# Cache pages fetched by direct DMAs of SyncE instead of GpSimd's indirect DMAs, and one output tile split into 512 and 64 columns

## The chip, the cores and the metric

One core of a Trainium2 chip runs the whole program. The engines are TensorE (PE; its weight loads are listed apart as PEld), VectorE (DVE), ScalarE (ACT), GpSimd (POOL) and SyncE (SP), which here only issues DMAs. The metric is the device time in microseconds (us); a kernel's time is the median of its runs.

## The reference

Two decoder layers (width 1024) run over 576 tokens: one prompt of 512, and 8 samples of 8 new tokens, each with 1024 past tokens in a paged cache. Cut to what matters here:

```
h = rmsnorm(x, ln_mix)
(hq, hf, hi, hog, dq, dk, dv, gq, gk, gv, gz, gb, ga, gate_a, gate_b, gate_c) = split(h @ w_in)
o_a = gated linear attention of hq, hf, hi          # 4 heads, "hg"
past_k, past_v = cache_k[l, page_table], cache_v[l, page_table]    # samples: 8 pages of 128 rows each
o_b = differential attention of dq, dk, dv over past and new tokens  # 4 heads, "df"; samples "ds"
o_c = gated delta rule of conv(gq, gk, gv)           # 4 heads, "gd"
mix = sigmoid(gate_a) * (o_a @ w_branch_a) + sigmoid(gate_b) * (o_b @ w_branch_b) + sigmoid(gate_c) * (o_c @ w_branch_c)
x = x + mix @ w_out
x = x + (silu(conv(g_ff)) * u_ff) @ w_down           # g_ff, u_ff = split(rmsnorm(x) @ w_up)
```

`page_table` [8, 8] holds numbers of 80 pages. A page of one layer is 128 rows of 512 floats (256 KB), for K (laid out feature by key) and for V. All states, new K and V rows and histories are outputs too.

## The kernel before

Activations lie feature-major: a tile is 128 features by 576 tokens. Every dense product is `dense_steps` (L264): for each of up to 8 tiles of the contraction it issues six matmuls of 288 columns each (weights split into a high and a low part, inputs too; three combinations, two halves of the tokens) into one PSUM accumulator of two banks. Its weights come as `raw` tiles of 128 x 512 floats (256 KB, four contraction tiles), loaded by SP at L274 into four rotating buffers; ACT casts the high part (L261), DVE subtracts for the low part (L194, `wl`). A raw buffer is thus used by 24 matmuls, and its next load waits for DVE's subtraction.

A layer has two parts. In the first, `drive` (L315) interleaves generators on three lanes (left, right and `smp`) with filling products. A generator yields an estimated time (us of planned PE time) after which its next PE step is to be placed, or asks for a dense product. The lanes left and right take the differential heads (df), then the delta-rule (gd) and linear heads (hg). The lane `smp` takes the decays, and after all df heads one `diff_sample` (L1256) per sample, then `diff_finish`. The filling products are eight gates of the heads and 24 branch gates, whose results are stored to DRAM (L716). PE runs in the order that comes of it. Program order and dependencies set the order of the other engines, each of which works strictly in its order; semaphores keep the data safe.

`diff_sample` fetches eight K pages in two tiles `pg` of four pages (two buffers in all, shared with V), multiplies the new keys (`sn`), waits 7.0, multiplies the scores of the first four pages and at once fetches the first four V pages into the buffer that this frees, waits 7.0, does the same for the second four, then the softmax, waits 7.5, transposes (yields 1.0, 1.0, 2.0), multiplies with V (32 matmuls per sample and one more group for the new values), and waits 1.2. Each page is one GpSimd indirect DMA (L1261), whose 128 row numbers stand in `idx` (L619, page number times 128 plus partition). A fetch waits for the matmuls that read the buffer last.

A delta-rule head sends a small tile through DRAM and back (`da`, `dtr`, `dt`, `ctt`, L849 to L864, all on SP). SP also loads states and stores results.

The second part is dense: the merge (L1376), the output projection (`w_out`, L1412), and the feed-forward network, with products of 288 columns throughout.

Of the kernel before, what the change touches and what calls it, by code (L numbers as in the profile page):

```python
# [22 lines left out]
SEQ = 512  # L23
# [122 lines left out]
def kernel(ctx, tc, a, o, depth=DEPTH, dbg=None):  # L146
# [15 lines left out]
    side = ['left']  # L162
    clk = [0.0]
# [32 lines left out]
    def params_load(l):  # L196
        """A layer's small parameters; the second part is loaded by the function that is returned."""
        fm = lay.tile([128, _FMN], F32, tag='fm', bufs=2, name='fm')
        nc.scalar.dma_start(fm, a['p_fm'][l])
        bcp = lay.tile([128, _BCN], F32, tag='bcp', bufs=2, name='bcp')  # L200
        hg = lay.tile([128, 12, 8, 3], F32, tag='hg', bufs=2, name='hg')

        def rest(eng):
            eng.dma_start(bcp, a['p_bc'][l].partition_broadcast(128))
            eng.dma_start(hg, a['hist_g'][l])

        return dict(F={k: fm[:, s:s + n] for k, (s, n) in _FMO.items()},
                    B={k: bcp[:, s:s + n] for k, (s, n) in _BCO.items()}, hg=hg), rest
# [41 lines left out]
    def rsqrt(out, v, n):  # L250
        """out = v ** -0.5 on [128, n] (v is kept)."""
        y, w = out, sm.tile([128, 20], F32, tag='rs_w', name='rs_w')[:, :n]
        V.tensor_scalar(out=y.bitcast(I32), in0=v.bitcast(I32), scalar1=1, scalar2=None, op0=ALU.logical_shift_right)
        V.tensor_scalar(out=y.bitcast(I32), in0=y.bitcast(I32), scalar1=-1, scalar2=0x5F3759DF, op0=ALU.mult, op1=ALU.add)
        for _ in range(3):
            tt(w, y, y, ALU.mult)
            V.scalar_tensor_tensor(out=w, in0=w, scalar=-0.5, in1=v, op0=ALU.mult, op1=ALU.mult)
            V.scalar_tensor_tensor(out=y, in0=w, scalar=1.5, in1=y, op0=ALU.add, op1=ALU.mult)
# [5 lines left out]
    def dense_steps(src, xs, M=128, raws=None, nk=None, prime=False):  # L264
        """src: dram [128, nk * M]; xs: [(xH, xL)] per k tile -> PSUM [M, 2, :288]; yields between k tiles.

        Weights are loaded, and split, ahead of their products; primed, it first yields when those of the first are."""
# [20 lines left out]
        for g, (k0, n) in enumerate(gr):  # L288
            wh, wl = nxt
            for i in range(n):  # L290
                if i == min(1, n - 1) and g + 1 < len(gr):
                    nxt = weights(g + 1)
                xh, xl = xs[k]
                cs = slice(i * M, (i + 1) * M)
                for w, xx in ((wh, (xh, xl)), (wl, (xh,))):
                    for hf in range(2):
                        for x_ in xx:
                            mm(acc[:M, hf, :HALF], w[:, cs], x_[:, hf * HALF:(hf + 1) * HALF],
                               start=(k == 0 and w is wh and x_ is xh), stop=(k == nk - 1 and w is wl))
                k += 1  # L300
                if k < nk:
                    yield
        return acc[:, :, :HALF]

    def dense(src, xs):
        return run(dense_steps(src, xs))
# [8 lines left out]
    def drive(stages, fill, xs, pre, psmp):  # L315
        """Interleaves stages (generators on two lanes) and filling products on the tensor engine.

        A stage yields a time to wait for its operands, ('mm', tile, src) for a product with xs, ('fill', key)
        for a filling product to have been done, or ('done', names) for stages to have ended."""
# [7 lines left out]
        def pick():  # L327
            """The next product: one that a stage waits for, or a filling one; its first weights are got ready."""
            while pend:
                ln, src = pend.pop(0)  # L330
                if ln is not None:
                    r = dict(ln=ln, key=None, post=None, gen=dense_steps(src, xs, prime=True), n=0)
                    break
                if src in fill:
                    r = filler(src)
                    break
            else:
                if not fill:
                    return None
                r = filler(next(iter(fill)))  # L340
            next(r['gen'])
            return r
# [75 lines left out]
    def norm_in(k, xt, g):  # L418
        """One tile of a normalised input, but for the tokens' norms: gained and split."""
# [17 lines left out]
    def norm_stats(sa, rb, r):  # L437
        """Reciprocal norms of the tokens: along the free axis on all partitions, and along partitions; in two parts."""
# [19 lines left out]
    def dense_with_stats(src, xs, sa, rb, rc):  # L458
        """A product with a normalised input, and the first part of the norms of its tokens on the way."""
# [6 lines left out]
    def transpose_to(dst, src, scale=None):  # L466
        """src [128, 576] feature-major -> dst [128, 5, 128] token-major, tokens scaled (rows 64: of the last tile zero)."""
# [13 lines left out]
    def transpose_back(src):  # L481
        """src [128, 5, 128] token-major -> two PSUM tiles: [128, 512] and [128, 64]."""
# [6 lines left out]
    def head_norm(ot, p):  # L489
        """rms-normalise [128, 5, 128] over the last axis, in place."""  # L490
# [21 lines left out]
    def sample_state(p, s0, eg, dst_dram, ktm, vrow, ve):  # L512
        """S' = e^{G} S0 + K^T V per sample; ktm [64, 128], vrow [64, 128]; eg [128, 8]."""
# [15 lines left out]
    def second(ap, m, e=1):  # L529
        """The columns of the second (or first) halves of the blocks of 2 m."""  # L530
        return ap.rearrange('p (n e m) -> p n e m', e=2, m=m)[:, :, e]

    def into(dst, ps, m):
        """Puts the corners of the blocks of 2 m, computed for the second halves' columns, into dst [128, 4, 128]."""
# [5 lines left out]
    # DRAM scratch  # L540
# [5 lines left out]
    # =========================== layers ===========================  # L546
    def params(l, r):
        """Works out what depends on a layer's small parameters alone."""
# [3 lines left out]
        # lambda  # L552
# [14 lines left out]
    def scalars_in(l, xt, g):  # L567
        """Inputs of the decay and beta scalars, four accumulations side by side."""
# [17 lines left out]
    with stage('ln0', 'right') as p0:  # L586
# [17 lines left out]
        # the masks, behind the input  # L604
# [13 lines left out]
    # page row indices: page * 128 + partition  # L618
    idx = cst.tile([128, NB * NPG], I32, name='idx')  # L619
    V.tensor_scalar(out=idx, in0=pt, scalar1=float(PAGE), scalar2=c['pidx'], op0=ALU.mult, op1=ALU.add)  # L620

    # forget lower bounds: cumulative softmax over layers minus the first layer's share
# [14 lines left out]
    for l in range(depth):  # L637
# [19 lines left out]
        def token_scalars(p):  # L657
            """Norms of the tokens, inputs of the scalars."""
# [49 lines left out]
        def half(dst, acc):  # L708
            """dst = acc / 2, normalised."""
# [16 lines left out]
        # =========================== delta rule heads ===========================  # L726
        def conv_silu(acc, ci, dst):
            """2 * silu of the causal width-4 convolution; dst [128, 576]."""
# [23 lines left out]
        def gdn_head(h, p):  # L752
# [7 lines left out]
            # token-major keys, norms of the keys  # L760
# [23 lines left out]
            def parts(i):  # L784
                """Rows of an exponent as three exact bfloat16 parts."""
# [9 lines left out]
            def weights(i, pc):  # L795
                """Decayed products of the keys with the keys (0) or the queries (1)."""
# [39 lines left out]
            # inverse of the unit triangular blocks of 16 by substitution, blocks on partitions  # L836
# [34 lines left out]
            # norms of the queries  # L871
# [16 lines left out]
            # token-major scaled values; scaled queries; the samples' keys and queries, each in its columns of 32  # L888
# [19 lines left out]
            for m in (16, 32, 64):  # L908
# [5 lines left out]
                # the second halves' columns of X are of no account  # L914
# [17 lines left out]
            # chunk recurrence  # L932
# [33 lines left out]
            # samples  # L966
# [22 lines left out]
        # =========================== gated linear heads ===========================  # L989
        def hgrn_head(h, p):  # L990
# [31 lines left out]
            # intra-chunk weights, level by level  # L1022
# [3 lines left out]
            def level(lhs, rhs, m):  # L1026
# [16 lines left out]
                # the columns are the second halves of the blocks  # L1043
# [9 lines left out]
            # pairs: the second token's decay is taken out of its key and put into its query  # L1053
# [24 lines left out]
            # decays  # L1078
# [51 lines left out]
        # =========================== differential attention ===========================  # L1130
# [125 lines left out]
        def diff_sample(b, p):  # L1256
            def pages(src, g):
                t = p.tile([128, 4, 512], F32, tag='pg', bufs=2, name='pg')
                for i in range(4):
                    k = NPG * b + 4 * g + i  # L1260
                    G.indirect_dma_start(t[:, i], None, src, bass.IndirectOffsetOnAxis(ap=idx[:, k:k + 1], axis=0))  # L1261
                return t

            Kp = [pages(a[f'kT{l}'], g) for g in range(2)]
# [10 lines left out]
            for g in range(2):  # L1275
                yield 7.0
                sc = rp()
# [3 lines left out]
                Vp.append(pages(a[f'v{l}'], g))  # L1281
# [7 lines left out]
            yield 7.5  # L1289
# [81 lines left out]
        # =========================== merge, output projection ===========================  # L1371
# [36 lines left out]
        with stage(f'ln2{l}', 'right') as p2:  # L1408
            sa = p2.tile([128, T], F32, tag='sqa', name='sqa')
            xs = []  # L1410
            for f in range(KD):
                acc = dense(a['w_out'][l, f], mixs)  # L1412
# [80 lines left out]
def _tiles(w, cols):  # L1493
    """[K, N] -> [len(cols), 128, K // 128 * 128]: blocks of 128 columns, rows on partitions."""
# [112 lines left out]
```

## Time and profile before

| | |
|---|---|
| time, median of 3 runs | 2508.27 us (2508.03 to 2509.12) |
| span of the profiled execution | 2624.5 us |
| TensorE matmul / weight load busy | 96% / 90% |
| DVE, ACT, POOL busy | 64%, 43%, 15% |
| mean granted clock of TensorE | 0.977 of full speed |
| DMA | 352.88 MB, 134 GB/s over the span; 67.13 MB by the software queue |

The profiled execution is one run with the recorder on; its span goes from the first to the last instruction and is longer than the timed runs. Busy shares are over the whole span, and PE's includes the modelled ends of matmuls, so what a stretch loses is read from tables by stretch and from the timeline. A row of the timeline gives the start, the length, the engine, the line (often that of a helper), the operation, the tiles (out<-in), the shapes and the count; in square brackets stands the idle time of the engine before it and what ended it. There "issue" means that nothing the profile shows was waited for, "remote" a release that it can't name.

### The profile page before, as it was taken

The page shows a single profiled execution, that of the slowest core. Times are in us where ns is not written, and L with a number is a line of the kernel's source. Part 1 is how long each engine was busy: PE and PEld are TensorE (multiplying, and loading weights), DVE is VectorE, ACT ScalarE, POOL GpSimd, SP SyncE. Part 2 cuts the span into 40 slices and gives each one's busy share as a digit, 9 for nine tenths or more (in the row PEclk, how much of TensorE's full clock was granted, in tenths as well). Part 3 has the DMA queues.
Part 4 walks back from the last instruction along what each step waited for, and adds up shares of the span by engine and source line. Part 5 has one row for each costly group of instructions (what it writes and reads, how often), then busy time and mean ns, then how long its engine had stood idle before and what let it go on. Part 6 is the DMA issues. An engine that isn't in the chain of part 4 may idle for free.

```text
span 2624.5 us, 51288 instructions
## 1 busy us (share of the span) xinstructions
PE 2528.1 (96%) x19714; PEld 2369.7 (90%) x19714; DVE 1677.0 (64%) x4219; ACT 1137.3 (43%) x2435; POOL 404.5 (15%) x634
## 2 busy tenths in 40 slices
PE   8999899899999999999999989989899999999999
PEld 7898778788999999999998887777789999999999
DVE  7777567477866564646677865656677666636464
ACT  5556455365542332323445554544455323323232
POOL 2001443341000010101010033444300000101010
PEclk8999899899999999999999999989899999999999
DMA  6234554544365424243442244546433654242423
GB/s 197 85 103 127 145 180 132 173 137 133 94 188 176 157 85 148 94 139 99 138 130 89 88 144 142 176 142 187 125 109 105 201 177 142 85 157 85 156 83 123
DMA packets 206453, 352.88 MB, mean 134 GB/s; under 512 B 36864, under 2 KB 71680, under 8 KB 206208
## 3 DMA queue, kind: packets, MB, share of 16 engines
q1 hardware_dynamic: 184144, 279.65, 33.7%
q0 software_dynamic: 20480, 67.13, 8.7%
q8 instruction: 156, 2.56, 0.4%
q10 hardware_dynamic: 1584, 2.82, 0.4%
q14 instruction: 89, 0.73, 0.1%
HBM read 288.90 MB, written 60.60 MB: 133 GB/s over the span
## 4 chain that ended last, share of the span: by engine, by line
PE 87%; DVE 5%; ACT 3%; another core or an unknown queue 2%; issue 2%; DMA 0%; ACTq 0%; SPq 0%; DVEq 0%
PE acc L187 70%; PE r L187 13%; PE r L191 4%; DVE mx L1216 1%; DVE wl L194 1%; ACT P L1219 0%; DVE ca L743 0%; DVE XX L194 0%; ACT wh L261 0%; DMA raw<-in_w_in_t 0%; DVE r L194 0%; ACT ks L777 0%; ACT ks L880 0%; ACT P L1286 0%
## 5 line engine op out<-in xcount | busy, mean ns | idle before, releaser
L187 PE MATMUL acc<-xh,wh 128*128 128x288 f32 x3584 | 1035.0, 303 | 1.0 <-issue 0.8
L187 PE MATMUL acc<-xl,wh 128*128 128x288 f32 x3584 | 1020.9, 300 | 3.8 <-issue 2.8
L187 PE MATMUL acc<-xh,wl 128*128 128x288 f32 x3584 | 779.2, 298 | 6.2 <-DVE wl L194 4.3
L261 ACT CAST wh<-raw 128x512 fp32r<-128x512 f32 x624 | 383.0, 615 | 843.5 <-PE acc L187 782.9
L187 PEld LDWEIGHTS acc<-xh,wh 128*128 128x128 f32 x3584 | 684.3, 191 | 24.2 <-issue 14.4
L187 PEld LDWEIGHTS acc<-xl,wh 128*128 128x128 f32 x3584 | 684.0, 191 | 10.1 <-issue 7.1
L187 PEld LDWEIGHTS acc<-xh,wl 128*128 128x128 f32 x3584 | 583.4, 191 | 11.0 <-DVE wl L194 6.3
L194 DVE TENSOR_TENSOR wl<-raw,wh 128x512 fp32r<-128x512 f32 x624 | 422.4, 679 | 189.8 <-ACT wh L261 187.3
L187 PE MATMUL acc<-hl,wh 128*128 128x288 f32 x704 | 197.5, 296 | 0.0
L187 PE MATMUL acc<-hh,wh 128*128 128x288 f32 x704 | 196.7, 294 | 0.0
L1261 POOL DMA_INDIRECT pg<-in_v,idx x128 | 153.8, 1202 | 121.9 <-PE r L187 84.6
L187 PE MATMUL acc<-hh,wl 128*128 128x288 f32 x704 | 150.7, 295 | 0.0
L1261 POOL DMA_INDIRECT pg<-in_kT,idx x128 | 129.2, 1009 | 133.3 <-PE r L187 95.2
L1442 POOL COPY fco<-cbf 128x2 f32<-128x2 f32 x44 | 30.3, 688 | 683.0 <-DVE cbf L194 683.0
L187 PEld LDWEIGHTS acc<-hh,wh 128*128 128x128 f32 x704 | 132.2, 188 | 0.0
L187 PEld LDWEIGHTS acc<-hl,wh 128*128 128x128 f32 x704 | 132.0, 188 | 0.0
L187 PEld LDWEIGHTS acc<-hh,wl 128*128 128x128 f32 x704 | 114.0, 189 | 0.0
L187 PE MATMUL acc<-oL,wh 128*128 128x288 f32 x384 | 108.0, 295 | 0.0
L187 PE MATMUL acc<-oh,wh 128*128 128x288 f32 x384 | 107.3, 295 | 0.0
L194 DVE TENSOR_TENSOR cbf<-acc,rb 128x288 f32<-128x288 f32 x132 | 39.0, 351 | 90.3 <-PE acc L187 86.3
L1448 DVE SCALAR_TENSOR_TENSOR caf<-cbf,fm,caf 128x592 f32<-128x592 f32 x88 | 73.5, 835 | 16.2 <-ACT caf L1446 14.6
L187 PE MATMUL acc<-oh,wl 128*128 128x288 f32 x384 | 81.6, 293 | 0.0
(418 smaller groups left out, 3858.3 us busy)
## 6 DMA issues: line engine op xcount, KB each, us to landing
raw<-in_w_in_t SPq DMA_DIRECT2D x272, 256.0 KB
raw<-in_w_up SPq DMA_DIRECT2D x176, 256.0 KB
raw<-in_w_dn SPq DMA_DIRECT2D x64, 256.0 KB
xo<-xres SPq DMA_DIRECT2D x56, 288.0 KB
thd<-thb SPq DMA_DIRECT2D x48, 288.0 KB
th<-thd SPq DMA_DIRECT2D x48, 288.0 KB
raw<-in_w_br SPq DMA_DIRECT2D x48, 256.0 KB
xres<-xn SPq DMA_DIRECT2D x32, 288.0 KB
```

What stands on the lines that cost most here:

```text
L187: PE.matmul(out, lhsT, rhs, start=start, stop=stop, **kw)
L191: PE.transpose(out, in_, idm)
L194: (eng or V).tensor_tensor(out=out, in0=in0, in1=in1, op=op)
L261: S.copy(hi, src)
L1216: V.tensor_reduce(out=mx[:, cc:cc + 1], in_=pss[cc][:, :nk], axis=AX.X, op=ALU.max)
L1261: G.indirect_dma_start(t[:, i], None, src, bass.IndirectOffsetOnAxis(ap=idx[:, k:k + 1], axis=0))
L1442: G.tensor_copy(fco[:, fi, 0, :], P[:, 512:514])
L1448: V.scalar_tensor_tensor(out=A[:, 0:592], in0=P[:, j:j + 592], scalar=w[:, 3 * fi + j:3 * fi + j + 1], in1=A[:, 0:592], op0=ALU.mult, op1= ...
```

## The change

Three things change; the rest of the difference is comments and docstrings taken out.

- `idx` and its computation go. `diff_sample` loads its eight page numbers from `pt` into SP registers, ordered behind the last page DMA that was issued (`lastp`), and fetches each page by a direct DMA of SP with the register as page number.
- The fetches move in the generator: from the second sample on the K pages come after a yield of 5.0; the first V pages after the second wait of 7.0, ahead of the second scores; the second V pages 5.0 after the softmax, and then a yield of 6.0 (before: 7.5 in all).
- The first `w_out` tile of the first layer splits the tokens as 512 and 64 instead of 288 and 288; its accumulator is read as one run of 576.

```diff
-    idx = cst.tile([128, NB * NPG], I32, name='idx')
-    V.tensor_scalar(out=idx, in0=pt, scalar1=float(PAGE), scalar2=c['pidx'], op0=ALU.mult, op1=ALU.add)
...
         def diff_sample(b, p):
-            def pages(src, g):
+            src = dict(K=a[f'kT{l}'].rearrange('(n p) e -> n p e', p=128), V=a[f'v{l}'].rearrange('(n p) e -> n p e', p=128))
+            with tc.issue_after(lastp[0].ins) if lastp else nullcontext():
+                _, page = nc.values_load_multi_w_load_instructions(pt[0:1, NPG * b:NPG * b + NPG], engines=[mybir.EngineType.SP], min_val=0, max_val=NPOOL - 1, bass_reorder=False)
+
+            def pages(what, g):
                 t = p.tile([128, 4, 512], F32, tag='pg', bufs=2, name='pg')
                 for i in range(4):
-                    k = NPG * b + 4 * g + i
-                    G.indirect_dma_start(t[:, i], None, src, bass.IndirectOffsetOnAxis(ap=idx[:, k:k + 1], axis=0))
+                    lastp[:] = [nc.sync.dma_start(t[:, i], src[what][bass.ds(page[4 * g + i], 1)].rearrange('o p e -> p (o e)'))]
                 return t
 
-            Kp = [pages(a[f'kT{l}'], g) for g in range(2)]
+            if b:
+                yield 5.0
+            Kp = [pages('K', g) for g in range(2)]
...
             for g in range(2):
                 yield 7.0
+                if g:
+                    Vp.append(pages('V', 0))
                 sc = rp()
...
-                Vp.append(pages(a[f'v{l}'], g))
...
-            yield 7.5
+            yield 5.0
+            Vp.append(pages('V', 1))
+            yield 6.0
...
-    def dense_steps(src, xs, M=128, raws=None, nk=None, prime=False):
+    def dense_steps(src, xs, M=128, raws=None, nk=None, prime=False, wide=False):
...
-                            mm(acc[:M, hf, :HALF], w[:, cs], x_[:, hf * HALF:(hf + 1) * HALF],
+                            ts = (slice(0, SEQ), slice(SEQ, T))[hf] if wide else slice(hf * HALF, (hf + 1) * HALF)
+                            mm(acc[:M, hf, :ts.stop - ts.start], w[:, cs], x_[:, ts],
...
+        if wide:
+            return acc.rearrange('p a b -> p (a b)')[:, 0:T].rearrange('p (a b) -> p a b', a=2)
...
-                acc = dense(a['w_out'][l, f], mixs)
+                acc = dense(a['w_out'][l, f], mixs, wide=(l, f) == (0, 0))
```

## Rows read from the trace of the kernel before

**Rows 1.** The page's busy time, and the granted clock in 40 slices.
```profile
PE 2528.1 (96%) x19714; PEld 2369.7 (90%) x19714; DVE 1677.0 (64%) x4219; ACT 1137.3 (43%) x2435; POOL 404.5 (15%) x634
...
PEclk8999899899999999999999999989899999999999
```
**Rows 2.** Stretches: length; busy us (instructions) of PE, PEld, DVE, ACT, POOL; clock; DMA share; GB/s.
```profile
60.00:230.00 170.00, 167.46 (x1218) 153.46 (x1218) 128.96 (x393) 93.14 (x252) 4.17 (x14) 1.00 0.31 99
230.00:610.00 380.00, 345.17 (x2940) 298.09 (x2939) 242.85 (x740) 190.63 (x435) 148.23 (x174) 0.93 0.51 153
610.00:737.00 127.00, 125.60 (x985) 114.07 (x983) 95.54 (x298) 67.73 (x180) 4.42 (x15) 1.00 0.36 108
757.00:777.00 20.00, 20.00 (x153) 20.00 (x153) 13.10 (x20) 10.29 (x17) 0.20 (x2) 1.00 0.78 239
1340.00:1525.00 185.00, 181.72 (x1328) 167.47 (x1327) 143.90 (x438) 99.81 (x267) 5.30 (x18) 1.00 0.31 97
1525.00:1910.00 385.00, 344.47 (x2951) 297.43 (x2950) 242.07 (x739) 190.05 (x436) 149.09 (x170) 0.93 0.50 150
```
**Rows 3.** Chain of waits, shares by line, of 230:610 and then of 60:230.
```profile
by line: PE acc L187 37.7%; PE r L187 28.8%; PE r L191 7.2%; another core or an unknown queue 6.7%; issue 5.3%; DVE ca L743 1.0%; ACT P L1286 1.0%; DMA ctt<-dt 0.9%; DMA dt<-dtr 0.9%; DVE XX L194 0.7%; DVE dd L809 0.6%; ACT wh L261 0.5%; DV
...
by line: PE acc L187 67.1%; PE r L191 9.5%; PE r L187 9.0%; DVE mx L1216 4.5%; ACT P L1219 2.8%; DVE r L194 1.8%; issue 1.5%; DVE P L1224 0.8%; DVE mx L1217 0.6%; DVE thb L710 0.4%; DVE thb L723 0.4%; DVE hx L710 0.4%; DVE wl L194 0.4%; DVE
```
**Rows 4.** Timeline of a run of eight K pages.
```profile
1757.61 0.95 POOL L1261 DMA_INDIRECT pg<-in_kT,idx  x1 [0.30 <-issue]
...
1758.86 0.94 POOL L1261 DMA_INDIRECT pg<-in_kT,idx  x1 [0.30 <-issue]
...
1761.31 1.58 PE L187 MATMUL r<-TB,X 128*128 128x64 f32 x8 [1.99 <-issue]
...
1766.41 0.44 DVE L536 COPY_PREDICATED TB<-cu,r 128x256 f32<-128x256 uint8 x1 [7.48 <-remote]
```
**Rows 5.** Timeline at the end of another such run, inside a dense product.
```profile
373.48 0.30 PE L187 MATMUL acc<-xl,wh 128*128 128x288 f32 x1 [0.76 <-issue]
...
374.92 0.29 PE L187 MATMUL acc<-xh,wl 128*128 128x288 f32 x1 [1.01 <-issue]
```
**Rows 6.** Stretches of half clock after 240 us, 16 in all: their sum.
```profile
sum 106.00, PE 86.70 PEld 74.97 DVE 24.05 ACT 32.37 POOL 46.23; mean PE 5.42 PEld 4.69 DVE 1.50 ACT 2.02 POOL 2.89
```
**Rows 7.** The page's groups of L1261; from the waits: total us, times, longest.
```profile
L1261 POOL DMA_INDIRECT pg<-in_v,idx x128 | 153.8, 1202 | 121.9 <-PE r L187 84.6
...
L1261 POOL DMA_INDIRECT pg<-in_kT,idx x128 | 129.2, 1009 | 133.3 <-PE r L187 95.2
...
POOL pg L1261 <- PE r L187: 179.8, 43, 15.3
```
**Rows 8.** Timeline, one weight load issued by SP.
```profile
1755.30 0.33 SPq L274 DMA_DIRECT2D raw<-in_w_in_t  x1
```
**Rows 9.** The page's DMA queues: packets, MB, share of 16 engines.
```profile
q0 software_dynamic: 20480, 67.13, 8.7%
```
**Rows 10.** Chain of waits in order of time: start, us, what.
```profile
441.70 3.35 DMA dt<-dtr
445.06 3.51 DMA ctt<-dt
...
749.02 152.24 PE acc L187 x1152
```
**Rows 11.** Lines L716 and L1331: durations ns, first and last start us.
```profile
L716 SPq DMA_DIRECT2D thd<-thb x48: 319/327/532, 199.4 to 2076.1; - x48
L716 SPq EVENT_SEMAPHORE  x32: 17/17/17, 207.2 to 2063.7; - x32
...
L1331 ACT ACTIVATE oTs<-r,dn x2: 472/474/475, 614.1 to 1912.4; 128x256 f32<-128x256 f32 x2
```
**Rows 12.** Timeline, eight products of 64 columns.
```profile
310.69 1.06 PE L187 MATMUL r<-XX 128*128 128x64 f32 x8
```
**Rows 13.** The page's costliest group: count, busy us, mean ns, idle before.
```profile
L187 PE MATMUL acc<-xh,wh 128*128 128x288 f32 x3584 | 1035.0, 303 | 1.0 <-issue 0.8
```

More of the change, by code (lines that the diff above doesn't have):

```diff
@@ L1 @@
 import math
-from contextlib import ExitStack
+from contextlib import ExitStack, nullcontext
 import numpy as np
@@ L162 @@
     side = ['left']
+    lastp = []
     clk = [0.0]
@@ L302, in dense_steps, with dense @@
                     yield
+        if wide:
+            return acc.rearrange('p a b -> p (a b)')[:, 0:T].rearrange('p (a b) -> p a b', a=2)
         return acc[:, :, :HALF]
-    def dense(src, xs):
-        return run(dense_steps(src, xs))
+    def dense(src, xs, wide=False):
+        return run(dense_steps(src, xs, wide=wide))
     def run(g):
```

## The prediction

> **What bounds the kernel now.** I read the page's busy row first: TensorE (PE) is busy 96% of the 2624.5 us span, and the clock row under it shows a 9 where the granted clock dips, so PE is the bound and only what it loses can be won [rows 1]. The busy-by-stretch table then says where it loses. While the attention samples run (230 to 610 us and 1525 to 1910 us, the stretches in which GpSimd is busy 148 us each) PE idles 34.8 and 40.5 us at a mean clock of 0.93; in the stretches around them it idles 2.5 of 170, 1.4 of 127 and 3.3 of 185 us, 1.5% together, at 1.00 [rows 2]. The chain of waits has the same contrast: "another core or an unknown queue" 6.7% and "issue" 5.3% inside, 1.5% of issue and none of the other outside [rows 3]. What PE stands at there is read from the timeline. Inside a run of eight GpSimd page fetches, one every 1.25 us, PE stands 1.99 us with nothing to wait for, and DVE is released 7.48 us after its last work, by something the profile can't name [rows 4]. Even plain accumulating matmuls, whose operands lie ready, stand 0.76 and 1.01 us at such a run's end [rows 5]. It isn't the bytes: from 757 to 777 us SP alone moves 239 GB/s, more than the 150 of the sample stretches, and PE is busy 20.00 of 20.00 us [rows 2].
>
> After each pause the clock falls: 16 stretches of half clock, 106.0 us, with PE busy in 86.7 of them [rows 6]. Half of that busy time, 43 us, is work that the full clock would have done.
>
> **The change, part by part.** *Fetches leave GpSimd.* 256 indirect DMAs go, about 1.0 and 1.2 us each [rows 7]. No compute engine waits for GpSimd by name, so its own 283 us are worth nothing; the pauses beside them are. Idle time over the background: 34.8 + 40.5 = 75.3, less 1.5% of the 765 us (11), leaves 64 us. Of it I keep a fifth (13 us), because the chain has DVE and ACT steps between the products that are late next once the pause is gone: 51 us. Clock: 43 us, less 5 for the falls behind a plain wait of PE for DVE: 38 us. Gain 89 us. Bounds: nothing, if direct fetches pause PE as well, and the full 64 + 43 = 107 us.
>
> *Fetches come to SP.* Each page is one direct DMA. SP's direct DMA takes 0.33 us to issue [rows 8], a page moves in 0.89 us (8.7% of the span over 256 pages [rows 9]). Eight K pages are thus 2.6 us of SP and 7.1 us of the 16 DMA engines; what stands behind them is the weight loads. Those have a cushion: four raw buffers, each consumed by 24 products; 1152 products took 152.24 us [rows 10], so a buffer lasts 3.2 us and a load is issued some three buffers, 9.5 us, ahead. 7.1 is under 9.5: nothing of it reaches PE. V pages come four at a time, 3.6 us, also under it. What has no cushion is the small round trip of the delta-rule heads (to DRAM, back, and again): 3.35 and 3.51 us on the chain [rows 10]. Sixteen such steps in all, perhaps a third behind a fetch of up to 7.1 us, and one in four on the chain: 5 us (0 to 16 x 7.1 = 114).
>
> *The new waits.* A page DMA waits for the buffer's last reader, as GpSimd did, and weight loads now queue behind SP's wait. GpSimd stood 179.8 us in 43 such waits, 4.2 us each [rows 7]. The change moves each fetch 5 to 7 us of planned PE time behind those readers, so I expect SP to find the buffer free: 0. Without that cover 4.2 us still lies inside the 9.5.
>
> *Register loads.* Eight page numbers per sample go into SP registers; no row shows this. Bounds per load: 0.017 us (an SP semaphore instruction [rows 11]) and 3.35 us (the small DMA round trip), that is 0.1 to 27 us of SP per sample. I take 0.5 us, as they are eight reads of one resident row, nearer to the instruction: 4 us per sample, inside the cushion; 4 us of PE in all for collisions. (The Trainium skill, "DMA: Bandwidth & Descriptors", section "Latency and other measured facts", puts such a load at a floor of about 0.6 us. By that eight take 4.8 us and the sum stays; no run here shows it yet.)
>
> *Longer samples.* The waits in the sample's generator grow from 26.7 to 35.2 planned us (+5, +5 + 6 - 7.5), 63 us per layer. That costs nothing while there is other work: the sample lane ends at 614 and 1912 us, but the gate products that fill PE run on to 773 and 2076 us [rows 11], past 749 us, where the heads' products have ended and plain ones begin [rows 10].
>
> *One w_out tile.* 24 pairs of 288 columns (0.132 us each) become 512 + 64. By width 0.235 + 0.029 us, nothing; but eight 64-column products took 1.06 us, 0.13 each [rows 12], so at most 24 x (0.235 + 0.13 - 0.264) = +2.4 us, and -0.5 if 512 columns go at one per cycle of 2.4 GHz. I take +1. The page index (one DVE instruction at the start) is nothing.
>
> **Sum.** -89 + 5 + 4 + 1 = -79, about -80 us of the 2624.5 us span, 3.05%. The runs' median, 2508.27 us, is 116 us below that span, so the recorded execution is stretched; I scale: 2508.27 x (1 - 80/2624.5) = 2432 us. Own range 2406 (the full 107 us, scaled, at no cost) to 2460 (50 us).
>
> **The rivals.** *Half the pauses stay* (0.13). Bursts of SP pages pause PE for a shorter time, or only the clock returns (38 us): about 35 us, 2475 (2460 to 2500). For it: the depth of a burst stays eight. Against: 239 GB/s from SP without a pause [rows 2].
>
> *The pauses aren't in the timed runs* (0.25). They stand in all engines at once and have no releaser, as if the recorder held the engines while GpSimd wrote its descriptors. 64 + 43 = 107 us is close to the 116 us by which the recording is longer. Then the fetch was hidden all along and 2508 stays, give or take 10 us for order: 2509. Against it: other places can hold the 116 us too; a 288-column product takes 0.132 us [rows 10] where 288 cycles of 2.4 GHz are 0.120, and the 3 x 3584 of the input products alone [rows 13] make 129 us of that. (The same result follows from a rule of the Trainium skill, "SBUF — State Buffer", section "Who interferes with whom": PE and ACT never wait on anyone, and a DMA never contends with a compute engine. By that rule removing GpSimd's fetches gives PE nothing. The trace speaks against it: 34.8 us of idle beside the fetches, none at 239 GB/s without them.)
>
> *Slower: the register loads are round trips* (0.13). If each of the eight waits for the one before at 3.35 us, SP stands 26.8 us per sample, 17.3 beyond the cushion, 16 times: +277 us; less the gain of 89, +188: about 2690. It decides from the load at which 16 x (8x - 9.5) exceeds 89, x = 1.9 us. For it: SP works strictly in order, and 9.5 us is all the weights have. Against: loads of neighbouring words need not wait for one another.
>
> *It doesn't do what it says* (0.06): direct bursts of eight pause PE just as much, and SP's lateness comes on top: 2508 + 5 + 4 + 1, some 2520.
>
> **How the numbers follow.** Forecast 0.43, half 0.13, recording 0.25 (0.08 faster, 0.13 same, 0.04 slower), register loads 0.13, not as said 0.06. About 0.2% (5 us) is what a measurement of this kernel can tell from none. Faster: 0.43 + 0.13 + 0.08 = 0.64, less 0.01 for the half case's edge, 0.63; same 0.14; slower 0.04 + 0.13 + 0.06 = 0.23. The range to be 8 in 10: 2405 to 2520 leaves out the register loads, part of the last case and a little below.
>
> **What would show it.** Right: no software queue in the DMA list, GpSimd under 130 us busy; in the sample stretches PE idle under 20 us each, clock 0.98 or more, "unknown queue" gone from the chain; the register loads' span on SP under 1 us each. Wrong: pauses of 1 to 3 us beside SP's page bursts; PE waiting for wl or wh (late weights) behind register loads; or a span shortened by 80 us whose timed runs don't follow, which is the recording rival. The w_out tile: 24 spacings of under 0.13 us.

## The result, and the profile after

| | before | after |
|---|---|---|
| time, median of 4 runs | 2508.15 us (2506.18 to 2509.12) | 2519.43 us (2517.85 to 2523.94) |
| span of the profiled execution | 2624.5 us | 2516.1 us (its own run: 2517.85 us) |

The change made the kernel slower by 0.5%: the ratio is 1.0052, with a 95% interval of 1.0038 to 1.0066. The forecast was 2432 us.

The profiled spans say the opposite: from 2624.5 to 2516.1 us, 108 us less. After's span is 1.75 us under the time of its own run; before's was 116 us over its timed runs. The page of after, which answers to [rows 1] and [rows 9]:

```profile
PE 2492.3 (99%) x19714; PEld 2338.6 (93%) x19714; DVE 1677.5 (67%) x4218; ACT 1134.2 (45%) x2435; POOL 119.3 (5%) x378
...
PEclk9999999999999999999999999999999999999999
...
q1 hardware_dynamic: 221008, 346.78, 42.3%
```

TensorE (PE) is busy 99%, no slice has a clock under 9, and the software queue is gone; its bytes are in the hardware queue. The table by stretch, which answers to [rows 2], same columns:

```profile
60.00:230.00 170.00, 167.44 (x1218) 153.60 (x1217) 128.28 (x383) 91.57 (x248) 5.52 (x21) 1.00 0.30 98
...
230.00:610.00 380.00, 376.90 (x3273) 328.81 (x3271) 280.43 (x841) 216.35 (x506) 17.03 (x58) 1.00 0.52 168
610.00:737.00 127.00, 126.24 (x1017) 116.68 (x1017) 89.71 (x261) 60.09 (x142) 1.28 (x5) 1.00 0.47 149
...
1525.00:1910.00 385.00, 381.78 (x3338) 335.65 (x3337) 283.06 (x865) 211.54 (x501) 14.59 (x50) 1.00 0.51 163
```

In the sample stretches PE idles 3.1 and 3.2 us, where it idled 34.8 and 40.5, at clock 1.00 instead of 0.93; the stretch without samples is as it was. The chain of waits of 230 to 610 us, as the first line of [rows 3], has no "unknown queue" any more:

```profile
by line: PE acc L188 54.6%; PE r L188 32.8%; PE r L192 6.3%; issue 1.2%; DMA pg<-in_v 0.9%; DVE wl L195 0.5%; ACT L746 0.3%; DVE G L1009 0.3%; DVE mx L1289 0.3%; ACT ks L880 0.3%; DVE xt L195 0.2%; DVE ca L743 0.2%; ACT ct L746 0.2%; DVE ap
```

So nearly every sign by which the forecast was to be known right is there (of the register loads on SP, below, the longest takes 1.20 us and not under 1), and the time went the other way. One sign of its being wrong is there too: a shorter span that the timed runs don't follow. Two things had to be found: where the 108 us of the trace are in the timed runs, and what costs the 11 us.

### The profile page after: what moved, and what is told of

The parts are those of the page before. It is cut to its first block, busy times and chain, and to the rows that moved or that the text cites. A ratio compares the mean times of both kernels' runs of the same rounds, so it can differ in the third digit from the quotient of the medians.

```text
span 2516.1 us, 52047 instructions
## 1 busy us (share of the span) xinstructions
PE 2492.3 (99%) x19714; PEld 2338.6 (93%) x19714; DVE 1677.5 (67%) x4218; ACT 1134.2 (45%) x2435; POOL 119.3 (5%) x378
## 4 chain that ended last, share of the span: by engine, by line
PE 93%; DVE 4%; ACT 2%; issue 1%; DMA 0%; SPq 0%; ACTq 0%; DVEq 0%
PE acc L188 75%; PE r L188 14%; PE r L192 4%; DVE mx L1216 1%; DVE wl L195 0%; ACT P L1219 0%; DVE r L195 0%; DMA x<-in_xT 0%; DVE mx L1289 0%; DMA pg<-in_v 0%; ACT ks L777 0%; DVE ca L743 0%; DVE thb L723 0%; DVE xl L427 0%; DVE ro L195 0%
## 5 line engine op out<-in xcount | busy, mean ns | idle before, releaser
L188 PE MATMUL acc<-xl,wh 128*128 128x288 f32 x3584 | 1010.7, 297 | 1.0 <-DVE xl L427 0.9
L188 PEld LDWEIGHTS acc<-xh,wh 128*128 128x128 f32 x3584 | 674.5, 188 | 33.8 <-issue 19.4
L188 PEld LDWEIGHTS acc<-xl,wh 128*128 128x128 f32 x3584 | 675.5, 188 | 6.4 <-issue 2.9
L188 PEld LDWEIGHTS acc<-xh,wl 128*128 128x128 f32 x3584 | 576.7, 188 | 11.9 <-DVE wl L195 6.5
L1412 DVE SCALAR_TENSOR_TENSOR xn<-acc,xo 128x576 f32<-128x576 f32 x40 | 30.3, 758 | 73.3 <-PE acc L188 73.3
L188 PEld LDWEIGHTS acc<-oL,wh 128*128 128x128 f32 x384 | 73.0, 190 | 0.0
L188 PE MATMUL acc<-mh,wh 128*128 128x288 f32 (+2 forms) x256 | 72.3, 296 | 0.0
```

The source lines that it names most:

```text
L188: PE.matmul(out, lhsT, rhs, start=start, stop=stop, **kw)
L1412: V.scalar_tensor_tensor(out=v2(xn), in0=acc, scalar=0.5, in1=v2(xo), op0=ALU.mult, op1=ALU.add)
```

## Experiments

Five sessions of runs followed, each on one chip with runs of the kernel before beside it. Its time is part of the finding:

| session | chip | before, median (range), runs |
|---|---|---|
| the result above | not recorded | 2508.15 (2506 to 2509), 4 |
| 1 | 4 | 2624.78 (2613 to 2632), 17 |
| 2 | 6 | 2629.62 (2625 to 2635), 11 |
| 3 | 6 | 2627.20 (2620 to 2640), 11 |
| 4 | 6 | 2627.55 (2618 to 2635), 12 |
| 5 | 6 | 2509.09 (2504 to 2512), 8 |

### Session 1: fetch and order taken apart

**c_before**: no edit.

> The kernel before, unchanged. Recording theory (the pauses beside GpSimd's fetches exist only while the detailed trace is taken): timed runs 2508 us +-4, each with a span about 2 us shorter than its time and a clock of 0.99 or more, while the execution that is traced again shows a span of 2600 to 2640 us with pauses in the sample stretches. Rival (the pauses are in every run, and direct fetches lose as much elsewhere): the spans and clocks of the timed runs are those of the trace, clock near 0.98.

2627.37 us (2617.5 to 2631.61), ratio to before 1.0004 (0.9986 to 1.0022). The profiled execution is one of the timed runs: 2630.08 us with a span of 2628.2. Its page:

```profile
PE 2530.6 (96%) x19714; PEld 2370.6 (90%) x19714; DVE 1676.9 (64%) x4219; ACT 1136.2 (43%) x2435; POOL 400.9 (15%) x634
...
PEclk9999899899999999999999999989899999999999
```

In session 1 the trace and the time agree, and both have the pauses. They are no artefact that only this trace has. Whether they were in the 2508 us is taken up below. One pause in the timeline of this kernel:

```profile
409.34 0.42 PE L187 MATMUL r<-Vs,PT 64*32 64x128 f32 x8
...
410.38 0.29 PE L187 MATMUL acc<-xl,wh 128*128 128x288 f32 x1
...
411.47 1.66 POOL L1261 DMA_INDIRECT pg<-in_kT,idx  x1 [0.30 <-issue]
...
413.43 0.95 POOL L1261 DMA_INDIRECT pg<-in_kT,idx  x1 [0.30 <-issue]
413.43 0.37 ACT L1310 ACTIVATE ob<-r,l 128x128 f32<-128x128 f32 x1 [4.76 <-remote]
...
414.11 0.47 PE L191 MATMUL r<-cf,ckq 128*128 128x128 f32 x1 [3.44 <-issue]
...
414.25 0.32 SPq L853 DMA_DIRECT2D dtr<-da  x1
```

ACT's `ob` waits for the products with `Vs`, which end at 409.8; it starts at 413.43, in the same instant as GpSimd's next fetch, whose forerunner took 1.66 us instead of 0.95. PE's next product follows at 414.11 and SP's next DMA at 414.25; for neither does the trace name a releaser. ACT, PE and SP go on within 0.9 us of each other.

**e_nowide**: after, without the wide tile.

```diff
-                acc = dense(a['w_out'][l, f], mixs, wide=(l, f) == (0, 0))
+                acc = dense(a['w_out'][l, f], mixs)
```

> The kernel after with the w_out tile split 288 and 288 again; the rest stays. If the wide tile is part of the loss (24 products of 512 columns at 0.284 us and 24 of 64 at up to 0.13, against 48 of 0.132): 2.5 us faster than after, some 2517. If fetch or order make the whole loss: 2518 to 2520.

2517.56 us (2514.94 to 2519.62), ratio 0.959 (0.9567 to 0.9614): some 2 us under after, near the first expectation (2517); the times alone hardly tell it from the second (2518 to 2520). The chain of plain products that holds the tile does: 153.12 us in after, 150.66 here, 1140 products in both.

**e_sp_old**: e_nowide with the fetches and waits at their places of before.

```diff
-            if b:
-                yield 5.0
...
-                if g:
-                    Vp.append(pages('V', 0))
...
+                Vp.append(pages('V', g))
...
-            yield 5.0
-            Vp.append(pages('V', 1))
-            yield 6.0
+            yield 7.5
```

> SP's direct fetches and register loads at the places and with the waits of the kernel before; w_out as before. Theory A (the new places in the order of PE's work cost the 11 us): 2508 +-3. Theory B (direct fetches on the SP queue, ahead of weight loads, cost them): 2518 or more, since the fetches now also stand on SP behind the buffer's readers, up to 2530.

2505.22 us (2503.78 to 2508.72), ratio 0.9545 (0.9522 to 0.9569). Theory A holds: with the old places the direct fetch costs nothing that can be seen. The new places cost 12.3 us (2517.56 - 2505.22). One thing is not held still here: although the places are those of before, PE's order in the trace differs from before's in 2622 of 19714 products.

**e_pool_new**: before, with K's wait of 5.0, the V pages and the waits moved as in after, fetched by GpSimd.

> GpSimd's indirect fetches at the new places with the new waits (K pages 5.0 later, V pages moved, 5.0 and 6.0 for 7.5); w_out as before. Theory A (order): 2518 +-3. Theory B (SP's queue): 2508 +-3. The recording theory expects of both that the trace shows a span about 110 us over the time, as in the kernel before; the rival expects no such gap where the fetches come later.

2649.75 us, ratio 1.0088 (1.0062 to 1.0114). Both numbers expected missed, since each took 2508 for granted; the sign of A is right (25 us more than before). Its span (2642.4) goes with its time (2644.21 in that run): the recording theory's gap of 110 us isn't there.

### Session 2: single parts, and what GpSimd's fetches cost

**e_sp_wide**: e_sp_old with the wide tile.

> SP's direct fetches at the old places (2505.22 us when it ran with the w_out tile split 288 and 288), with the w_out tile split 512 and 64. If the wide tile costs what its rows say (24 products of 512 columns at 0.284 us and 24 of 64 for 48 of 0.132): +2.5 us, some 2507.7. If it is hidden: 2505.

2509.64 us (2506.29 to 2513.16). It ran on another chip than e_sp_old, so the 4 us are not sure; the chains are. Here stand start, length and count of the same stretch of plain products, first in e_sp_wide, then in e_sp_old's second run:

```profile
685.38 154.70 PE acc L188 x1152
```
```profile
686.59 152.23 PE acc L188 x1152
```

The tile costs 2.47 us.

**e_sp_k5**: e_sp_old with `if b: yield 5.0` ahead of the K pages alone.

> SP's direct fetches with the wait of 5.0 ahead of the K pages alone, V pages and the other waits as in the kernel before, w_out as before. If that wait makes the cost of the new order (12 us against 2505.22): 2515 or more. If the moved V pages and the longer wait ahead of the transposes make it: 2505 to 2508.

2525.19 us (2522.42 to 2527.31): 20 us over e_sp_old, 8 more than all parts of the new order together.

**e_k_sp_v_pool**: e_sp_old with the V pages by GpSimd.

```diff
+                    if what == 'V':
+                        k = NPG * b + 4 * g + i
+                        G.indirect_dma_start(t[:, i], None, a[f'v{l}'], bass.IndirectOffsetOnAxis(ap=idx[:, k:k + 1], axis=0))
+                        continue
```

> K pages by SP's direct DMAs, V pages by GpSimd's indirect ones, all at the old places; w_out as before. If the pauses go by the number of indirect DMAs (128 instead of 256, 2625 against 2505): half, 2565 +-15. If only the bursts of eight (K) make them: 2510 or less. If a state of the chip or the session makes them, before will be near 2508 where this is near 2505, and near 2625 where this is above 2540.

2525.11 us, ratio 0.9614 (0.9595 to 0.9633). Half of the indirect DMAs, 20 us of 120: neither the half expected nor the 2510 or less.

**e_pool_narrow**: before, with rows of 64 floats.

```diff
-                    G.indirect_dma_start(t[:, i], None, src, ...
+                    G.indirect_dma_start(t[:, i, 0:64], None, src, ...
```

> The kernel before with its 256 indirect DMAs, each fetching 64 of a row's 512 floats (7 of 8 parts of every page are left out and stand as zeros): the same 128 descriptors each, an eighth of the bytes. If the pauses come with the descriptors that GpSimd writes: 2615 to 2635, as before. If they come with the bytes of the software queue: 2520 or less.

2648.88 us, ratio 1.0067 (1.005 to 1.0085). An eighth of the bytes, PE's order as in before, and slower than either expectation: the bytes are not it.

### Session 3: after again, and two orders

**after_again**: no edit.

> The kernel after, unchanged, beside the kernel before on one chip. If the 2508 us of before and the 2519 of after were taken alike and the pauses were a matter of the recording alone: before and after 11 us apart again, after the slower. If GpSimd's fetches cost time whenever the pauses show (before at 2625 and 2630 us in the two studies so far): after 2519 +-4, before 2620 to 2632, a ratio of 0.958.

2518.57 us (2518.01 to 2523.26), as in the result's session; before beside it 2627.20: ratio 0.9596 (0.958 to 0.9613). The same change is 0.5% slower in one session and 4.0% faster in another, and it is before that differs.

**e_sp_old2**: e_sp_old again.

> SP's direct fetches at the old places, w_out as before, a second time (2505.22 us the first time, on another chip): 2505 +-3 if its lead of 12 us over the new order is the order's; 2515 or more if it was the chip's.

2505.64 us (2504.7 to 2508.94). The lead over after on one chip in one session is 12.9 us; without the wide tile's 2.5, the order costs 10.4 here.

**e_sp_vnew**: e_nowide without K's wait of 5.0.

> SP's direct fetches with the V pages at the new places and the longer wait ahead of the transposes, but without the wait of 5.0 ahead of the K pages; w_out as before. If the parts of the new order add up (K's wait +20 us over 2505, all of it +12): 2497. If any order but the old costs 10 to 20 us, as it happens to fall: 2510 to 2525.

2523.19 us (2520.19 to 2525.27). The parts don't add up: K's wait alone +20, the V places alone +18, both +12.

**e_pool_k44**: e_pool_new without K's wait of 5.0, and with the second four K pages fetched after the first wait of 7.0.

> GpSimd's 256 indirect DMAs, but never more than four in a row: the second four K pages come after the first wait of 7.0, the V pages at the new places. If runs of eight make the pauses (V by GpSimd alone, in fours, cost 20 us and not 60): 2560 or less, the trace with under 45 us of idle TensorE. If each indirect DMA adds its share: 2615 to 2650.

2651.62 us, ratio 1.0095 (1.0076 to 1.0113). It didn't do what it was for. GpSimd's timeline still has eight K pages in a row, since both buffers come free at once (first and last of such a run):

```profile
321.68 0.94 POOL L1261 DMA_INDIRECT pg<-in_kT,idx  x1 [12.98 <-PE r L187]
...
330.43 0.94 POOL L1261 DMA_INDIRECT pg<-in_kT,idx  x1 [0.30 <-issue]
```

### Session 4: runs of eight

**e_k_pool_v_sp**: as e_k_sp_v_pool, with `what == 'K'` and K's tensor.

> K pages by GpSimd's indirect DMAs (eight in a row), V pages by SP's direct ones, old places, w_out as before: the counterpart of the run with K by SP and V by GpSimd (2525). If runs of eight make the pauses: 2590 to 2625, TensorE idle 70 us or more over the span. If any 128 indirect DMAs cost the same 20 us and only all 256 together cost 120: 2520 to 2535.

2622.27 us, ratio 0.999 (0.9975 to 1.0005): the whole loss with 128 of the 256 DMAs. The rows of 230 to 610 us, here and with V by GpSimd (columns as in [rows 2]):

```profile
230.00:610.00 380.00, 343.28 (x2943) 297.90 (x2941) 241.66 (x739) 189.18 (x434) 71.01 (x106) 0.93 0.50 152
```
```profile
230.00:610.00 380.00, 373.16 (x3329) 325.62 (x3328) 277.92 (x853) 216.34 (x508) 95.36 (x124) 1.00 0.55 168
```

**e_pool_split**: before, with the V products in two parts, so that the page buffers come free apart.

```diff
             for i in range(9):
+                if i == 4:
+                    yield 9.0
```

> The kernel before, its 256 indirect DMAs kept, with a wait of 9.0 between the products of the first four V pages and those of the second four, so that the two page buffers come free apart and GpSimd's K pages go four and four (the run meant to do this by moving the fetch left them eight in a row). If runs of eight make the pauses: 2560 or less. If the K pages' share does not depend on that: 2610 to 2650.

2572.48 us, ratio 0.9796 (0.9772 to 0.9819). This time the K pages do go in fours (last of four, then first of the next four):

```profile
322.33 0.95 POOL L1261 DMA_INDIRECT pg<-in_kT,idx  x1 [0.30 <-issue]
331.31 0.94 POOL L1261 DMA_INDIRECT pg<-in_kT,idx  x1 [8.03 <-PE r L187]
```

In the trace 24 runs of four K pages and 4 of eight are left. Within a run or up to 5 us behind it, PE idles 10.4 us in all for the 24 and 7.4 for the 4, so K pages in fours cost what V pages in fours do, about 0.4 us a run. 2572 lies between the 2560 and the 2610 that were to divide the theories, with the order of PE's work changed by the split as well; e_sp_split, below, is the counterpart that takes this out.

**e_pool_rows32**: before, with 32 rows per fetch.

```diff
-                    G.indirect_dma_start(t[:, i], None, src, ...ap=idx[:, k:k + 1], axis=0))
+                    G.indirect_dma_start(t[0:32, i], None, src, ...ap=idx[0:32, k:k + 1], axis=0))
```

> The kernel before with 256 indirect DMAs of 32 rows instead of 128 (96 rows of every page are left out and stand as zeros), eight in a row as before: a quarter of the descriptors. If the pauses go by descriptors: 2540 or less. If they go by instructions of GpSimd: 2615 to 2650, as with the narrow rows (2649).

2663.78 us, ratio 1.014 (1.0113 to 1.0166). A quarter of the rows, PE's order as in before, and more than the range expected, not less.

**e_sp_y8**: e_sp_old with `yield 8.0` for the two `yield 7.0`.

> SP's direct fetches at the old places, with the two waits of 7.0 ahead of the scores set to 8.0 and nothing else changed. If the lead of the old places over the three other orders tried (2505 against 2518, 2525 and 2523) is the way TensorE's work happens to interleave: 2512 to 2526. If only the fetches' places matter: 2505 +-3.

2520.05 us (2518.41 to 2522.43): 15 us for a microsecond more on each of two waits, with no fetch moved in the program.

### Session 5: the counterparts

**e_sp_split**: e_sp_old with the edit of e_pool_split.

> SP's direct fetches at the old places with the same split of the V products (a wait of 9.0 between the first four pages and the second four): the counterpart of GpSimd's fetches with that split (2572 us; its trace has 46.6 us of idle TensorE against 19 with SP's fetches, and 48 us of half clock against 3 to 10). If pauses and the clock behind them are all that GpSimd's fetches cost: 2572 - 28 - 20 = 2524 +-5. If direct fetches cost something of their own: 2535 or more.

2524.64 us (2520.1 to 2527.69), with before at 2509.09: ratio 1.0065 (1.0045 to 1.0086). The number came as expected, the account behind it only in part. The sums of the two sample stretches (765 us; busy PE first), of e_pool_split and of e_sp_split:

```profile
sum 765.00, PE 733.02 PEld 631.88 DVE 527.06 ACT 397.55 POOL 272.35; mean PE 366.51 PEld 315.94 DVE 263.53 ACT 198.78 POOL 136.18
```
```profile
sum 765.00, PE 758.14 PEld 659.49 DVE 558.86 ACT 422.49 POOL 31.68; mean PE 379.07 PEld 329.75 DVE 279.43 ACT 211.25 POOL 15.84
```

25 us of idle PE, and half of 46.1 less 24.7 us of half clock, 11, make 36 us. The traced executions lie 41 us apart (2564.7 and 2523.6), so 5 are not accounted for; the medians lie 48 apart because e_pool_split's traced run was its fastest (2566.5). The runs are of different sessions, but kernels with direct fetches don't show the session (after: 2519.43 and 2518.57).

**e_sp_y6**: e_sp_old with `yield 6.0`.

> SP's direct fetches at the old places, the two waits of 7.0 ahead of the scores set to 6.0. A fifth order: if the interleaving as it falls decides, anywhere from 2505 to 2526; if shorter waits are better in themselves (8.0 cost 15 us), under 2505.

2517.00 us (2516.6 to 2519.38), ratio 1.0038 (1.0023 to 1.0052). Longer and shorter both lose.

## Why the prediction was wrong

**The step that failed is the base of the sum.** The text noted that the median lay 116 us below the span, read it as an execution that recording stretches evenly, and scaled: 2508.27 x (1 - 80/2624.5). The 116 us were the pauses themselves and the half clock behind them. The trace was of an execution as in sessions 1 to 4, the times of runs as in session 5, and a gain of 89 us was taken off times that did not hold it. Every run of the five sessions has a span and a granted clock of its own on record: before's clock is 0.973 to 0.982 in sessions 1 to 4 and 0.997 to 1.000 in session 5. So at 2509 us the half clock that follows the pauses is all but gone. The runs of 2508 us have no clock on record; that they were like those of session 5 is read from their time. With 116 us next to a bound of 107, the numbers were at hand. What was set against the rival, that 288 columns take 0.132 us and not 0.120, proves nothing: with direct fetches the products take as long (1140 in 150.66 us in e_nowide), and after's span and time differ by 1.75 us.

**The recording rival** (0.25, 2509 us give or take 10) missed by 0.4 us (2519.43). Its mechanism is shown only in part. That before's timed runs were free of the pauses is supported by session 5, as above. That recording makes the pauses is not shown: all of c_before's timed runs show them in their clocks, and the runs of session 5, whose spans and clocks were taken as well, do not. On chip 6 before took 2627 to 2630 us in three sessions and 2509 in one, so it isn't the chip. In the four sessions at 2627 other kernels with GpSimd's fetches ran beside before, in the two at 2508 none did; whether that is the cause, these runs don't tell, and no trace of before at 2508 us exists. It stays open.

The nearest number belongs to *it doesn't do what it says* (0.06, some 2520; its terms add up to 2518), and that was luck: PE idles 3.1 and 3.2 us in the sample stretches beside the direct bursts, so they don't pause it, and SP's lateness costs nothing that can be seen.

**Gain 89 us** (idle 51, clock 38): too small, and so was the bound of 107. After's span is 108.4 us under before's with the costs of order and tile in it. e_sp_old, which has neither, is 121.0 us under (2624.5 less 2503.5). Its page:

```profile
span 2503.5 us, 51999 instructions
...
PE 2479.2 (99%) x19714; PEld 2332.3 (93%) x19714; DVE 1676.9 (67%) x4218; ACT 1139.1 (46%) x2435; POOL 118.7 (5%) x378
```

PE's idle time falls from 96.4 to 24.3 us, its busy time from 2528.1 to 2479.2. The fifth that was held back went too, and two stretches of half clock ahead of 240 us were not in the 43 us. In session 3 the gain is there in the times: 2627.20 to 2505.64 for e_sp_old, to 2518.57 for after. Runs of eight fetches, not GpSimd's work as such, make most of it: added up in c_before's trace, idle PE within a run or up to 5 us behind it is 67 us for 16 runs of eight K pages and 12 us for 27 runs of four V pages.

(The Trainium skill, "SBUF — State Buffer", section "Who interferes with whom", says that PE never waits on anyone. The prediction weighed it and sided with the trace. At 2508 us the rule gave the better number; at 2627 PE stands 37.2 of 380 us beside these runs (342.83 busy in c_before, 230 to 610 us).) The largest wait of PE that c_before's trace puts down to an engine is for ACT, below two that it can put down to nothing (us, times, longest, over the span):

```profile
PE r L191 <- issue: 16.6, 8, 5.1
PE r L187 <- issue: 14.3, 7, 3.3
PE r L191 <- ACT ks L880: 10.8, 5, 3.5
```

**Fetches on SP, +5, and new waits, 0**: right, nearer to 0. With the old places direct fetches give 2505.2 and 2505.6 us, where before without pauses has 2508 and 2509 (PE's order is not the same, as said). The rows of the waits, after, for SP's page DMAs and for PE's late weights (us, times, longest):

```profile
SPq L1264 <- PE r L188: 104.4, 41, 10.3
```
```profile
PE acc L188 <- DVE wl L195: 5.3, 4, 2.0
```

That SP would find the buffers free was wrong: it stands 104 us for them, up to 10.3 at a time. That the weights' cushion covers it was right: PE waits 5.3 us for late weights in all, against 4.3 before.

**Register loads, +4**: mis-sized, and without effect. One load fetches all eight numbers, and two short instructions per number follow; the rows give shortest, median and longest in ns:

```profile
L1259 SPq FUSED_REGOPS  x128: 147/147/178, 30.5 to 1807.9; - x128
L1259 SPq SEQ_ASSERT  x128: 18/18/33, 30.7 to 1808.1; - x128
L1259 SPq TENSOR_LOAD <-pt x16: 533/720/1202, 25.0 to 1801.6; - x16
```

That is 0.72 us per sample for the load and, with eight times 0.147 and 0.018 for the rest, 2.0 us of SP, not 4. (The Trainium skill, "DMA: Bandwidth & Descriptors", "Latency and other measured facts", has a floor of about 0.6 us for such a load. The median here, for eight numbers together, is near it; the shortest, 0.53 us, is under it.) The rival of round trips, 2690 us, is refuted.

**Longer samples, 0**: wrong, and the term that decides the sign. The cover was there: after the samples, from 610 to 737 us, PE is busy 126.24 of 127 us in after. But the yields set how the small products and the dense ones are interleaved on PE, and the new places cost 12.3 us by that (e_nowide against e_sp_old). The old places have 2505; six other orders tried with direct fetches have 2517 to 2525. Little of it is idle time: 24 to 30 us over the span in the six, 24 in e_sp_old. Start and length of the next long chain of each layer, in e_sp_old and in e_nowide:

```profile
846.22 412.40 PE acc L188 x3132
...
2090.33 409.25 PE acc L188 x3108
```
```profile
852.72 412.40 PE acc L188 x3132
...
2100.78 409.25 PE acc L188 x3108
```

6.5 us are lost by the end of the first layer's mix and 3.9 in the second's; the chains themselves are the same to the hundredth. Counted in the traces, PE changes between dense (`acc`) and small (`r`) products 785 times in e_sp_old and 825 in e_nowide, and the step into a dense product takes 0.105 and 0.125 us on average (41.3 and 51.8 us in all); the differences of the other steps add up to about nothing. In the five other orders it is 809 to 853 changes. That the changes cause the loss is not shown, and their number alone does not decide it: before's order has 829, and before takes 2508 and 2509 us without pauses. An estimate of PE's busy time at full clock (busy time less half of what falls in stretches of half clock) gives 2479 us for e_sp_old, 2479 and 2483 for the traces of before and c_before, and 2485 to 2492 for the six orders. Which of the neighbours on PE cost that time stays open.

**The w_out tile, +1** (up to +2.4): +2.47, and +2.46 between after and e_nowide. The timeline of after (start, us) has the first four matmuls:

```profile
793.25 0.39 PE L188 MATMUL acc<-mh,wh 128*128 128x512 f32 x1
793.48 0.40 PE L188 MATMUL acc<-ml,wh 128*128 128x512 f32 x1
793.71 0.20 PE L188 MATMUL acc<-mh,wh 128*128 128x64 f32 x1
793.75 0.28 PE L188 MATMUL acc<-ml,wh 128*128 128x64 f32 x1
```

512 columns are followed after 0.23 us here, but over the 24 after 0.284 on average; that size was off.

**The 11.3 us**, then: fetch -3 (2505.2 against 2508.15, two sessions), order +12.3, tile +2.5, together +11.8. The first term is from different sessions and holds a change of PE's order as well.

**What is best.** e_sp_old, direct fetches at the old places, is 12.9 us faster than after in one session and 4.5% faster than before where the pauses are (0.9545, 0.9529 to 0.9562). Against before without them its 3 us, 0.1%, are from different sessions and too little to tell.

## What to carry to other kernels

When a traced execution is longer than the timed runs by about the loss that the change is to win back, time the kernel before again beside the trace ahead of forecasting anything: the loss may not be in the times. Leave the order of a tuned instruction stream alone when an engine's fetch is swapped, look in the trace whether it stayed (here PE's order changed with the fetches at their old places), and measure a moved wait by itself: a microsecond more or less on each of two waits cost 12 to 15 us here. Whole pages at table numbers can be fetched by direct DMAs with one register load per eight pages; such kernels had the same time in both sessions in which each ran (after 2519.43 and 2518.57, e_sp_old 2505.22 and 2505.64).

## What the runs showed of the hardware

- The same kernel took 2504 to 2512 us in one session, at a granted clock of 0.997 to 1.000, and 2618 to 2640 in three others on the same chip, at 0.973 to 0.981; after, whose fetches are SP's, took 2519.43 us in a session with before at 2508 us and 2518.57 in one with before at 2627.
- Runs of eight indirect DMAs, 1.25 us apart, cost PE about 4 us of idle time each, runs of four 0.4. An eighth of the bytes (2648.88 us) or a quarter of the rows (2663.78) did not lessen it. Why such a run holds up other engines is not shown.
